# Layer 1's sliding-window scores: fp32 matmuls on 32-row tiles in place of stacked high and low halves, with the value projection moved to second place

## The chip, the cores and the metric

The kernel runs on one core of a Trainium2 chip. Its time is the device time of one execution in microseconds (us); three executions took 1122.43, 1123.97 and 1125.91 us, median 1123.97 us. The profile was taken of a further execution of 1124.34 us, whose span on the core is 1122.6 us. Engines are called as the profile calls them: PE (TensorE, matmuls), PEld (its weight loads), DVE (VectorE), ACT (ScalarE), POOL (GpSimd), SP (which issues most DMAs).

## The reference, cut to what matters

One inference step of a two-layer decoder for 256 prompt rows and 64 sample rows, all in float32. The part that is changed is layer 1's sliding-window attention over the prompt: 16 query heads in 4 groups per key head, 4 key heads, head size 64, window 128, with a learned sink per head.

```python
qp, kp, vp = odd_qkv(hp, pos_p, w_qkv_o[j], b_qkv_o[j])          # projection, bias, rotary on q and k
op = window_attn_prompt(qp, kp, vp, sinks[j]) @ w_out_o[j] + b_out_o[j]
...
def sink_attention(q, k, v, valid, sinks):
    s = jnp.einsum('...qkgd,...skd->...kgqs', q, k).astype(jnp.float32) * (C_HEAD_DIM ** -0.5)
    s = jnp.where(valid, s, -jnp.inf)
    sink = jnp.broadcast_to(sinks.astype(jnp.float32).reshape(C_KV_HEADS, C_GROUP, 1, 1), s.shape[:-1] + (1,))
    p = jax.nn.softmax(jnp.concatenate([s, sink], axis=-1), axis=-1)[..., :-1]
    return jnp.einsum('...kgqs,...skd->...qkgd', p.astype(v.dtype), v)
```

The 256 prompt queries are two blocks of 128. A query of block n sees keys of block n and of block n-1; block 0 has no block before it.

## The kernel before, in words

**Projections.** Every weight matrix is read in pieces of 128 x 2048 from one array (`ws`), in the order of a list (`plan`), through three `stage` buffers. Each piece is split into a high half rounded to fp32r (`whi`, written by ACT) and the rest (`wlo`, subtracted by DVE), in two parts of 1024 columns with four buffers each. The activations are split in the same way (`XH`, `XL`; later `HH`, `HL`). `gemm2` multiplies one piece with three fp32r matmuls per product (high x high, high x low, low x high), 48 matmuls a call, and calls `evac` at its end; `gemm_tok` does the same with positions on the partitions (24 matmuls per 512-wide piece, 64 for the value projection `w_qkv 5`). When a piece starts, the next one is split.

**Hooks.** Side work is put between the matmuls of the projections: `hook(i, f, j)` runs f inside the i-th following call, after the j-th of its 16 steps (a step is 3 matmuls in `gemm2`). PE, DVE, ACT and POOL each work through their own list strictly in the order that the compiled program has, so an instruction that waits holds all behind it on that engine. The order on each engine is made when the program is built, from priorities and an estimate of readiness.

**Layer 1, in the order of the program.** `qk_group(4)` makes the keys (one half of each head's 64 features on a chunk: chunk 8 holds features 0-31 of the four key heads in four bands of 32 partitions, chunk 9 features 32-63), `qk_group(0..3)` the queries of group g of all four key heads (chunks 2g, 2g+1 of the tile `QA`, called `k` in the profile since it lies in the buffer `k10`). Its `evac` scales on DVE (2 `t<-mm,RB`), rotates (4 `t<-t,cv,cst` on DVE, a subtract and an add `k<-t,t` on POOL). Then `gemm_tok` makes the values `VW` (in the buffer `cst`).

**Scores.** `stack_k` and `stack_q` build operands with 128 rows out of the 64 features: first `hilo` (ACT rounds, DVE subtracts), then ACT and DVE copy bands of 32 partitions so that one band holds a high half, the next a low half. For the keys this is the tile `khl` (buffer `k8b`), for the queries `sq` (buffer `Z`). A head's scores are then two fp32r matmuls of 128 rows and 256 columns (`at<-k8b,Z`). `w1` is one unit of 2 or 4 heads: matmuls into `at` banks (four PSUM banks), `tensor_tensor_reduce` on DVE (mask and row maximum; CUSTOM_DVE_ANT_0 in the profile, ISA in the program), `sink_softmax` (ACT exponentials, small DVE operations, DVE scaling). `w2f` transposes the probabilities on PE (`at<-ident,w`), `w3` multiplies them with the values (`at<-w,cst`), and ACT and DVE write high and low halves of the result to `OH`, `OL`. There are 12 units, in slots of two: slot i runs `w3` of the units two slots back, `w2f` of those one slot back, `w1` of its own. The slots lie in hooks from the value projection on, through `mem1.mk(0..3)` (memory keys, 48 matmuls of 256 columns each) and the pieces of `mem1.mv` (memory values, 24 matmuls of 512 columns each). `ws_prep`, `ws_scores`, `ws_tr`, `ws_pv` are the sample rows' attention; they stay as they are.

Of the kernel before, what the change touches and what calls it, by code (L numbers as in the profile page):

```python
# [9 lines left out]
F32 = mybir.dt.float32  # L10
F32R = mybir.dt.float32r
I32 = mybir.dt.int32
AF = mybir.ActivationFunctionType
# [62 lines left out]
def decoder_step(ctx: ExitStack, tc: tile.TileContext, d, plan):  # L76
# [968 lines left out]
    m1 = coc("m1")  # L1045
    VW = cst1[:, COW:COW + 768].rearrange("p (b c) -> p b c", b=3)
    bv = coc("bv")
    khl = sb([P, 2, 4, 256], "k8b", 1, F32R)

    def qk_group(g):  # L1050
        def evac(ps):
# [13 lines left out]
            V.scalar_tensor_tensor(q, zb, bb, cosw, op0=ALU.add, op1=ALU.mult)  # L1065
            G.tensor_tensor(QA[:, 2 * g + 1], p, q, op=ALU.add)
        gemm2(("w_qkv", g), nm.h, nm.l, NT, evac)

    def hilo(src, w):
        hi = sb([P, 512], "w2", W2, F32R)[:, :w]  # L1070
        lo = sb([P, 512], "w2", W2, F32R)[:, :w]
        if len(src.shape) == 3:
            hi = hi.rearrange("p (g t) -> p g t", g=src.shape[1])
            lo = lo.rearrange("p (g t) -> p g t", g=src.shape[1])
        A.activation(hi, src, AF.Copy)
        V.tensor_tensor(lo, src, hi.bitcast(F32), op=ALU.subtract)
        return hi.bitcast(F32), lo.bitcast(F32)

    def stack_k():
        for f in range(2):  # L1080
            hl = hilo(QA[:, 8 + f, :NPR], NPR)
            for kv in range(4):
                r = slice(32 * kv, 32 * kv + 32)
                for x in range(2):
                    for du in range(2):
                        q = (f + 2 * du) * 32
                        if du:
                            V.tensor_copy(khl[q:q + 32, x, kv], hl[x][r])
                        else:
                            A.activation(khl[q:q + 32, x, kv], hl[x][r], AF.Copy)  # L1090

    sq_t = {}

    def stack_q(gp, fs=(0, 1)):
        if 0 in fs:
            sq = sb([P, 2080], "Z", 1, F32R)[:, :2048].rearrange("p (k g t) -> p k g t", k=4, g=2)
            sq_t[gp] = sq
        sq = sq_t[gp]
        for f in fs:
            hl = hilo(QAv[:, 2 * gp:2 * gp + 2, f, :NPR], 512)  # L1100
            for kv in range(4):
                r = slice(32 * kv, 32 * kv + 32)
                for x in range(2):
                    q = (f + 2 * x) * 32
                    if x:
                        V.tensor_copy(sq[q:q + 32, kv], hl[x][r])
                    else:
                        A.activation(sq[q:q + 32, kv], hl[x][r], AF.Copy)

    isc = 0.125  # L1110
    OH = sb([P, KC, NT], "HH", 2, F32R)
# [2 lines left out]
    def sink_softmax(s, nh, mx, nsk, sk, sums, per):  # L1114
        nm_ = sb([P, nh], "w_nm", 4)
        es = sb([P, nh], "w_es", 4)
        if per:
            V.scalar_tensor_tensor(nm_, mx, -isc, nsk, op0=ALU.mult, op1=ALU.min)
        else:
            V.tensor_scalar(nm_, mx, -isc, nsk, op0=ALU.mult, op1=ALU.min)  # L1120
        for h in range(nh):
            A.activation(s[:, h], s[:, h], AF.Exp, bias=nm_[:, h:h + 1], scale=isc, accum_out=sums[:, h:h + 1])
        if per:
            V.tensor_tensor(es, nm_, sk, op=ALU.add)
            A.activation(es, es, AF.Exp)
# [7 lines left out]
    units = []  # L1133
    for gp in range(2):
        for pr in range(2):
            units.append((0, gp, pr, None))
        for kv in range(4):
            units.append((1, gp, kv // 2, kv))
    us, up_, uo = {}, {}, {}

    def w1(u):
        n, gp, pr, kv = units[u]
        heads = [(k, g) for k in ((2 * pr, 2 * pr + 1) if n == 0 else (kv,)) for g in range(2)]
        nh = len(heads)
        kw = 512 // nh
        s = sb([P, 512], "w2", W2).rearrange("p (h k) -> p h k", k=kw)
        mx = sb([P, nh], "w_mx", 4)
        msk = m1[:, P:256] if n == 0 else m1
        for j, (k, g) in enumerate(heads):
            if j % 2 == 0:  # L1150
                sp = bank("at")
            o = (j % 2) * 256
            for x in range(2):
                T.matmul(sp[:, o:o + 256], sq_t[gp][:, k, g, n * P:(n + 1) * P], khl[:, x, k],
                         start=(x == 0), stop=(x == 1))
            V.tensor_tensor_reduce(out=s[:, j], in0=sp[:, o:o + kw], in1=msk, op0=ALU.add, op1=ALU.max,
                                   scale=1.0, scalar=NEG, accum_out=mx[:, j:j + 1])
        sums = sb([P, nh], "w_sm", 4)
        if n == 0:
            for i in range(2):  # L1160
                i0 = CV["sink_p"][0] - CV["sink_s"][0] + (2 * pr + i) * 4 + 2 * gp
                sink_softmax(s[:, 2 * i:2 * i + 2], 2, mx[:, 2 * i:2 * i + 2], nsink[:, i0:i0 + 2],
                             cvc("sink_p", (2 * pr + i) * 4 + 2 * gp, 2), sums[:, 2 * i:2 * i + 2], True)
        else:
            i0 = CV["sink_p"][0] - CV["sink_s"][0] + kv * 4 + 2 * gp
            sink_softmax(s, 2, mx, nsink[:, i0:i0 + 2], cvc("sink_p", kv * 4 + 2 * gp, 2), sums, True)
        us[u] = s

    def w2f(u):
        n, gp, pr, kv = units[u]  # L1170
        s = us.pop(u)
# [8 lines left out]
        up_[u] = pt  # L1180

    def w3(u):
        n, gp, pr, kv = units[u]
        pt = up_.pop(u)
        first = n == 0 or kv % 2 == 0
        if first:
            uo[n, gp, pr] = bank("at")
        po = uo[n, gp, pr]
        for i in range(2):
            k = 2 * pr + i if n == 0 else kv  # L1190
            ro = slice((k % 2) * 64, (k % 2) * 64 + 64)
            kb = 0 if n == 0 else i
            T.matmul(po[ro, :256], VW[:, kb, k * 64:(k + 1) * 64], pt[:, i * 256:(i + 1) * 256],
                     start=(n == 0 or i == 0), stop=(n == 0 or i == 1))
        if n == 0 or kv % 2 == 1:
            src = po[:, :256].rearrange("p (g q) -> p g q", g=2)
            c0 = pr * 4 + 2 * gp
            oh = OH[:, c0:c0 + 2, n * P:(n + 1) * P]
            A.activation(oh, src, AF.Copy)
            V.tensor_tensor(OL[:, c0:c0 + 2, n * P:(n + 1) * P], src, oh.bitcast(F32), op=ALU.subtract)  # L1200

    sm_ = {}

# [81 lines left out]
    def slot(i):  # L1285
        for u in (2 * i - 4, 2 * i - 3):
            if 0 <= u < 12:
                w3(u)
        for u in (2 * i - 2, 2 * i - 1):
            if 0 <= u < 12:  # L1290
                w2f(u)
        for u in (2 * i, 2 * i + 1):
            if u < 12:
                w1(u)

    def rows_out():
        G.dma_start(d["wk_p"], QA[:, 8:10, P:2 * P])
        G.dma_start(d["wk_n"], QA[:, 8:10, NPR:NT])
        G.dma_start(d["wv_p"], VW[:, 1])
        G.dma_start(d["wv_n"], VW[64:128, 2])  # L1300

    qk_group(0)
    hook(0, stack_k)
    qk_group(1)
    hook(0, lambda: stack_q(0, (0,)))
    hook(1, lambda: stack_q(0, (1,)))
    qk_group(2)
    qk_group(3)
    hook(0, lambda: slot(0))
    gemm_tok([("w_qkv", 5)], nm.h, nm.l, XS, 256, evac)  # L1310
    hook(0, lambda: slot(1), rows_out)
    hook(1, lambda: slot(2), lambda: stack_q(1))
    hook(2, ws_prep, lambda: slot(3))
    hook(3, lambda: slot(4))
    for g in range(4):
        mem1.mk(g)
    hook(0, lambda: slot(5), lambda: ws_scores(0))
    hook(1, lambda: slot(6), lambda: ws_scores(1))
    hook(2, lambda: slot(7), lambda: ws_tr(0))
    hook(3, lambda: ws_tr(1), j=3)  # L1320
    hook(3, ws_pv, j=11)
    mem1.mv(0)
# [47 lines left out]
def _plan():  # L1370
# [243 lines left out]
```

## Time and profile before

| what | value |
|---|---|
| runs | 1122.43, 1123.97, 1125.91 us (median 1123.97) |
| profiled execution | 1124.34 us, span 1122.6 us |
| PE busy | 1086.4 us, 97% of the span |
| DVE, ACT, POOL busy | 738.8 (66%), 524.2 (47%), 136.3 us (12%) |
| layer 1 from the end of its norm to the last `mem1.mv` matmul | 634.95 to 759.64 us of the span |
| DVE busy from 640 to 660 us | 19.77 of 20.00 us |

PE is busy nearly all the time, so the time of the kernel is PE's list of matmuls plus the places where PE stands still or runs at half its clock. The profile writes an fp32 matmul as two records, an fp32r matmul as one; a record's own duration contains a tail that overlaps the next one, so what a matmul costs is read from the distance between starts. "Idle" in brackets is the time that an engine stood before an instruction, and the name behind the arrow what ended it.

### The profile page before, as it was taken

The page shows a single profiled execution, that of the slowest core. Times are in us where ns is not written, and L with a number is a line of the kernel's source. Part 1 is how long each engine was busy: PE and PEld are TensorE (multiplying, and loading weights), DVE is VectorE, ACT ScalarE, POOL GpSimd, SP SyncE. Part 2 cuts the span into 40 slices and gives each one's busy share as a digit, 9 for nine tenths or more (in the row PEclk, how much of TensorE's full clock was granted, in tenths as well). Part 3 has the DMA queues.
Part 4 walks back from the last instruction along what each step waited for, and adds up shares of the span by engine and source line. Part 5 has one row for each costly group of instructions (what it writes and reads, how often), then busy time and mean ns, then how long its engine had stood idle before and what let it go on. Part 6 is the DMA issues. An engine that isn't in the chain of part 4 may idle for free.

```text
span 1122.6 us, 18500 instructions
## 1 busy us (share of the span) xinstructions
PE 1086.4 (97%) x7424; PEld 1021.9 (91%) x7424; DVE 738.8 (66%) x1447; ACT 524.2 (47%) x910; POOL 136.3 (12%) x131
## 2 busy tenths in 40 slices
PE   7998999999999999999999989999999999999996
PEld 7886979999987999999999988879968999999995
DVE  8999885776545575555556898956536855555543
ACT  6454641545325355444445557745323654343432
POOL 4506030123000010000001222002000200000001
PEclk9999999999999999999999989999999999999998
DMA  9432337744787644444444334547576444444421
GB/s 349 146 128 98 131 119 271 287 148 152 296 328 309 263 151 150 151 150 151 150 151 150 121 113 156 188 149 278 209 300 264 149 150 151 150 151 150 151 75 48
DMA packets 30982, 201.55 MB, mean 180 GB/s; under 512 B 3624, under 2 KB 4792, under 8 KB 7992
## 3 DMA queue, kind: packets, MB, share of 16 engines
q1 hardware_dynamic: 27584, 187.13, 45.8%
q0 software_dynamic: 2512, 11.54, 2.8%
q10 hardware_dynamic: 800, 1.70, 0.5%
q8 instruction: 58, 0.95, 0.3%
q14 instruction: 28, 0.23, 0.1%
HBM read 187.51 MB, written 12.85 MB: 178 GB/s over the span
## 4 chain that ended last, share of the span: by engine, by line
PE 74%; DVE 13%; DMA 5%; ACT 4%; issue 2%; POOL 1%; SPq 0%; ACTq 0%; DVEq 0%; POOLq 0%
PE mm L64 64%; PE at L64 10%; DVE wlo L64 5%; DMA stage<-ws 4%; DVE t L64 2%; ACT whi L64 2%; DVE w L64 1%; POOL t L64 1%; DVE XL L64 1%; ACT w L64 1%; ACT k L64 1%; DVE Z L64 0%; DVE k8b L64 0%; DVE nw_u L64 0%; DVE X L64 0%
## 5 line engine op out<-in xcount | busy, mean ns | idle before, releaser
L64 DVE TENSOR_TENSOR wlo<-stage,whi 128x1024 fp32r<-128x1024 f32 (+1 forms) x270 | 339.5, 1264 | 191.6 <-ACT whi L64 189.9
L64 ACT ACTIVATE whi<-stage 128x1024 fp32r<-128x1024 f32 (+1 forms) x270 | 280.2, 1050 | 363.5 <-PE mm L64 273.4
L64 PE MATMUL mm<-HH,whi 128*128 128x320 f32 (+1 forms) x960 | 294.4, 308 | 2.2 <-ACT HH L64 2.2
L64 PE MATMUL mm<-HL,whi 128*128 128x320 f32 (+1 forms) x960 | 293.8, 306 | 0.3 <-DVE HL L64 0.2
L64 PE MATMUL mm<-HH,wlo 128*128 128x320 f32 (+1 forms) x960 | 293.3, 306 | 0.0
L64 PE MATMUL mm<-XH,whi 128*128 128x320 f32 x912 | 286.9, 315 | 5.3 <-ACT whi L64 5.3
L64 PE MATMUL mm<-XH,wlo 128*128 128x320 f32 x912 | 283.9, 311 | 5.5 <-DVE wlo L64 5.3
L64 PE MATMUL mm<-XL,whi 128*128 128x320 f32 x912 | 283.4, 311 | 0.0
L64 PEld LDWEIGHTS mm<-HH,whi 128*128 128x128 f32 x960 | 180.7, 188 | 4.9 <-ACT HH L64 2.4
L64 PEld LDWEIGHTS mm<-HL,whi 128*128 128x128 f32 x960 | 181.0, 189 | 1.0 <-DVE HL L64 0.8
L64 PEld LDWEIGHTS mm<-HH,wlo 128*128 128x128 f32 x960 | 180.9, 188 | 0.1
L64 PEld LDWEIGHTS mm<-XH,whi 128*128 128x128 f32 x912 | 172.8, 189 | 6.9 <-ACT whi L64 5.3
L64 PEld LDWEIGHTS mm<-XH,wlo 128*128 128x128 f32 x912 | 172.6, 189 | 6.7 <-DVE wlo L64 6.7
L64 PEld LDWEIGHTS mm<-XL,whi 128*128 128x128 f32 x912 | 172.8, 189 | 0.7
L64 POOL TENSOR_TENSOR ssq<-ssq,sqt 128x320 f32<-128x320 f32 x39 | 41.6, 1068 | 609.0 <-ACT sqt L64 608.1
L64 DVE TENSOR_TENSOR X<-mm,X 128x320 f32<-128x320 f32 x112 | 51.7, 488 | 56.8 <-PE mm L64 56.6
L64 ACT ACTIVATE t<-t 128x320 f32<-128x320 f32 x88 | 38.0, 462 | 24.1 <-DVE t L64 24.1
L64 DVE SCALAR_TENSOR_TENSOR t<-mm,RB 128x320 f32<-128x320 f32 x64 | 30.1, 491 | 25.5 <-PE mm L64 22.6
L64 ACT ACTIVATE HH<-t 128x320 fp32r<-128x320 f32 x80 | 34.5, 462 | 21.6 <-DVE t L64 21.1
L64 DVE TENSOR_TENSOR HL<-t,HH 128x320 fp32r<-128x320 f32 x80 | 37.0, 491 | 9.9 <-ACT HH L64 9.3
L64 DVE SCALAR_TENSOR_TENSOR XL<-X,cv,XH 128x320 fp32r<-128x320 f32 x48 | 38.4, 822 | 4.7 <-ACT XH L64 4.7
L64 ACT ACTIVATE XH<-X,cv 128x320 fp32r<-128x320 f32 x48 | 26.3, 554 | 21.1 <-DVE X L64 19.3
(240 smaller groups left out, 1139.3 us busy)
## 6 DMA issues: line engine op xcount, KB each, us to landing
stage<-ws SPq DMA_DIRECT2D x162, 1024.0 KB, 4.8
o_ret_s<-stage POOLq DMA_DIRECT2D x8, 512.0 KB, 6.9
HH<-ws SPq DMA_DIRECT2D x4, 1024.0 KB, 6.8
HL<-ws SPq DMA_DIRECT2D x4, 1024.0 KB, 6.6
k8a<-ws SPq DMA_DIRECT2D x2, 1024.0 KB, 8.3
o_mem_k<-k8a POOLq DMA_DIRECT2D x2, 1024.0 KB, 8.2
o_mem_v<-k8b POOLq DMA_DIRECT2D x2, 1024.0 KB, 10.6
cst<-ce SPq DMA_DIRECT2D x1, 1296.0 KB, 10.3
```

The costliest lines, as they stand in the source:

```text
L64: r = f(*a, **k)
```

## The change

Nothing is split and stacked any more. The scores are plain fp32 matmuls straight from `QA`: for one group g and one half f, four matmuls, one for each key head, each with 32 rows (its band of partitions) and 128 weight columns, into a bank of their own; f = 0 and f = 1 accumulate. `w1` now does all four key heads at once, in three calls: block 1 with groups 0 and 1, block 0 with all four groups, block 1 with groups 2 and 3. It takes all four `at` banks, and its softmax writes to one big tile (`k8b`, `Z`, `k8b`). Block 0 computes 128 columns of scores where it had computed 256 and read 128. `w3` handles two key heads at once. The value projection is second in the plan, before the queries, and the hooks are laid out anew.

```diff
-    khl = sb([P, 2, 4, 256], "k8b", 1, F32R)
...
-    def hilo(src, w):
-        hi = sb([P, 512], "w2", W2, F32R)[:, :w]
-        lo = sb([P, 512], "w2", W2, F32R)[:, :w]
...
-        A.activation(hi, src, AF.Copy)
-        V.tensor_tensor(lo, src, hi.bitcast(F32), op=ALU.subtract)
...
-    def stack_k():
-        for f in range(2):
-            hl = hilo(QA[:, 8 + f, :NPR], NPR)
...
-    def stack_q(gp, fs=(0, 1)):
...
-            hl = hilo(QAv[:, 2 * gp:2 * gp + 2, f, :NPR], 512)
...
-    def w1(u):
...
-            for x in range(2):
-                T.matmul(sp[:, o:o + 256], sq_t[gp][:, k, g, n * P:(n + 1) * P], khl[:, x, k],
-                         start=(x == 0), stop=(x == 1))
...
+    def w1(n, gp, tag):
+        gs = range(4) if n == 0 else (2 * gp, 2 * gp + 1)
+        kw = 512 // len(gs)
+        sp = [bank("at") for _ in range(4)]
+        for j, g in enumerate(gs):
+            for f in range(2):
+                for kv in range(4):
+                    r = slice(32 * kv, 32 * kv + 32)
+                    T.matmul(sp[kv][:, j * kw:(j + 1) * kw], QAv[r, g, f, n * P:(n + 1) * P], QA[r, 8 + f, :kw],
+                             start=(f == 0), stop=(f == 1))
+        big = sb([P, 2080 if tag == "Z" else 2048], tag)
...
+        for kv in range(4):
+            s = big[:, kv * 512:(kv + 1) * 512].rearrange("p (h k) -> p h k", k=kw)
...
+    def w3(n, gp, pr):
+        po = bank("at")
+        ng = 4 if n == 0 else 2
+        w = ng * P
+        pts = [up_.pop((n, gp, 2 * pr + i)) for i in range(2)]
+        for kb in range(n + 1):
+            for i in range(2):
+                k = 2 * pr + i
+                T.matmul(po[i * 64:i * 64 + 64, :w], VW[:, kb, k * 64:(k + 1) * 64], pts[i][:, kb * w:(kb + 1) * w],
+                         start=(kb == 0), stop=(kb == n))
...
-    qk_group(0)
-    hook(0, stack_k)
-    qk_group(1)
-    hook(0, lambda: stack_q(0, (0,)))
-    hook(1, lambda: stack_q(0, (1,)))
-    qk_group(2)
-    qk_group(3)
-    hook(0, lambda: slot(0))
     gemm_tok([("w_qkv", 5)], nm.h, nm.l, XS, 256, evac)
-    hook(0, lambda: slot(1), rows_out)
...
+    hook(2, lambda: w1(1, 0, "k8b"), j=9)
+    hook(3, lambda: w2f(1, 0, 0), lambda: w2f(1, 0, 1), j=9)
+    hook(4, lambda: w3(1, 0, 0), lambda: w2f(1, 0, 2), lambda: w2f(1, 0, 3), rows_out, j=3)
+    hook(4, lambda: w1(0, 0, "Z"), j=13)
+    hook(5, lambda: w3(1, 0, 1), ws_prep, j=5)
+    hook(6, lambda: w2f(0, 0, 0), lambda: w2f(0, 0, 1), j=3)
...
+    hook(7, lambda: w1(1, 1, "k8b"), j=9)
+    for g in range(4):
+        qk_group(g)
     for g in range(4):
         mem1.mk(g)
...
-    p += [("w_qkv", 4), ("w_qkv", 0), ("w_qkv", 1), ("w_qkv", 2), ("w_qkv", 3), ("w_qkv", 5)]
+    p += [("w_qkv", 4), ("w_qkv", 5), ("w_qkv", 0), ("w_qkv", 1), ("w_qkv", 2), ("w_qkv", 3)]
```

On PE, before, the first scores stand inside the value projection (`mm` from `whi`, `wlo` and `XH`, `XL`); each row here is one unit's pair of heads, and its operands are the stacked tiles.

```order
L64 MATMUL mm_6683<-wlo_6599,XH_5982 128x256
L64 MATMUL mm_6683<-whi_6598,XL_5983 128x256
L64 MATMUL at_6721<-k8b_6217,Z_6545 128x256 x2
L64 MATMUL at_6728<-k8b_6217,Z_6545 128x256 x2
L64 MATMUL at_6760<-k8b_6217,Z_6545 128x256 x2
L64 MATMUL at_6767<-k8b_6217,Z_6545 128x256 x2
L64 MATMUL mm_6682<-whi_6602,XH_5982 128x256
```

Now they stand inside `qk_group(2)`, 30 of whose 48 matmuls are ahead of them: 16 matmuls in one block (this row of four, four times over), with `QA` (`k`) as both operands and a bank for each key head.

```order
L64 MATMUL mm_6563<-XL_5983,whi_6484 128x320
L64 MATMUL mm_6563<-XH_5982,wlo_6485 128x320
L64 MATMUL at_6594<-k_945_6216 128x256
L64 MATMUL at_6595<-k_945_6216 128x256
L64 MATMUL at_6596<-k_945_6216 128x256
L64 MATMUL at_6597<-k_945_6216 128x256
```

The scores moved from behind all four query groups to the middle of the third, and no longer read `k8b` and `Z`.

On DVE, before, this is what stands ahead of the first scores: the evacuation of `qk_group(2)`, the low half of the stacked queries (`w<-k`), splits of weights (`wlo`) and the copies to `Z`.

```order
L64 TENSOR_TENSOR wlo_6603<-stage_6596,whi_6602 128x1024
L64 SCALAR_TENSOR_TENSOR t_1014_6592<-t_1010_6583,cv_62,cst_6211 128x320
L64 TENSOR_TENSOR w_1023_6633<-k_945_6216,w_1022_6632 128x512
L64 TENSOR_TENSOR wlo_6688<-stage_6685,whi_6687 128x1024
L64 CAST Z_6545<-w_1023_6633 32x512 x4
L64 TENSOR_TENSOR t_1024_6668<-mm_6606,RB_6329 128x320
```

Now, ahead of the first scores and behind them, with the evacuation of `qk_group(1)` first and the softmax of block 1 (ISA rows) last:

```order
L64 TENSOR_TENSOR t_998_6538<-mm_6488,RB_6329 128x320
L64 TENSOR_TENSOR t_999_6539<-mm_6489,RB_6329 128x320
L64 SCALAR_TENSOR_TENSOR t_1000_6542<-t_998_6538,cv_62,cst_6211 128x320
L64 SCALAR_TENSOR_TENSOR t_1001_6543<-t_999_6539,cv_62,cst_6211 128x320
L64 SCALAR_TENSOR_TENSOR t_1002_6547<-t_998_6538,cv_62,cst_6211 128x320
L64 TENSOR_TENSOR wlo_6559<-stage_6552,whi_6558 128x1024
L64 SCALAR_TENSOR_TENSOR t_1003_6548<-t_999_6539,cv_62,cst_6211 128x320
L64 TENSOR_TENSOR wlo_6710<-stage_6707,whi_6709 128x1024
L64 ISA k8b_6614,w_mx_6615<-at_6594,cst_6211 128x256
```

The subtractions and copies are gone from this list, and DVE goes from an evacuation straight to the softmax.

On POOL, now, `ws_prep` (MEMSET and COPY of `XH`) lies between and around the two operations that finish the queries of group 3 (`t_1051` to `t_1054`), behind those of group 2:

```order
L64 TENSOR_TENSOR k_945_6216<-t_1036_6702,t_1037_6703 128x320
L64 MEMSET XH_7041 128x2048
L64 TENSOR_TENSOR k_945_6216<-t_1051_6785,t_1052_6786 128x320
L64 COPY XH_7041<-k_945_6216 32x8x32 x4
L64 TENSOR_TENSOR k_945_6216<-t_1053_6790,t_1054_6791 128x320
L64 COPY XH_7041<-k_945_6216 32x8x32 x4
```

Before, all ten `k<-t,t` of POOL came ahead of this MEMSET and its copies.

## Rows read from the trace of the kernel before

**Rows 1.** The page: each engine's busy time, share, instructions.
```profile
PE 1086.4 (97%) x7424; PEld 1021.9 (91%) x7424; DVE 738.8 (66%) x1447; ACT 524.2 (47%) x910; POOL 136.3 (12%) x131
```
**Rows 2.** Waits of PE, 634.6 to 759.6: us in total, times, longest.
```profile
PE at L64 <- DVE Z L64: 4.7, 2, 3.8
PE at L64 <- DVE w_mx L64: 1.1, 1, 1.1
PE mm L64 <- DVE t L64: 0.7, 1, 0.7
```
**Rows 3.** Stretches: us, busy PE, PEld, DVE, ACT, POOL, PEclk, DMA, GB/s.
```profile
640.00:660.00 20.00, 20.00 (x139) 20.00 (x138) 19.77 (x38) 15.40 (x27) 6.60 (x7) 1.00 0.32 107
661.55:664.50 2.95, 2.95 (x24) 2.89 (x24) 2.95 (x5) 2.90 (x4) 1.12 (x1) 1.00 0.01 3
668.46:674.35 5.89, 5.89 (x26) 5.67 (x26) 5.80 (x11) 0.00 (x0) 1.13 (x2) 0.51 0.11 45
819.40:842.40 23.00, 22.23 (x239) 13.87 (x242) 10.46 (x48) 7.75 (x26) 0.00 (x0) 1.00 0.81 315
```
**Rows 4.** PE in order of time: start, us, instruction [idle before].
```profile
634.95 0.55 PE L64 MATMUL mm<-XH,whi 128*128 128x320 f32 x1
...
668.46 0.77 PE L64 MATMUL at<-k8b,Z 128*128 128x256 f32 x2 [3.82 <-DVE Z L64]
...
707.18 1.45 PE L64 MATMUL at<-k8b,Z 128*128 128x256 f32 x10
708.48 0.28 PE L64 MATMUL mm<-HH,whi 128*128 128x256 f32 x1
...
819.43 1.93 PE L64 MATMUL at<-stage,Z 128*32 128x256 f32 x32
821.29 3.72 PE L64 MATMUL at<-k8a,k 128*128 128x256 f32 x16
```
**Rows 5.** DVE in order of time, ahead of the first scores.
```profile
667.90 0.87 DVE L64 CAST Z<-w 32x512 fp32r<-32x512 f32 x2
```
**Rows 6.** Groups on DVE, 636 to 710: count | busy us, mean ns | idle.
```profile
L64 DVE TENSOR_TENSOR wlo<-stage,whi 128x1024 fp32r<-128x1024 f32 x14 | 22.6, 1619 | 0.5 <-ACT whi L64 0.4
L64 DVE SCALAR_TENSOR_TENSOR t<-t,cv,cst 128x320 f32<-128x320 f32 x20 | 10.1, 545 | 0.0
L64 DVE CAST Z<-w 32x512 fp32r<-32x512 f32 x16 | 6.7, 420 | 0.4
L64 DVE TENSOR_TENSOR t<-mm,RB 128x320 f32<-128x320 f32 x10 | 4.4, 484 | 1.5 <-ACT RB L64 1.4
L64 DVE CUSTOM_DVE_ANT_0 w<-at,cst 128x256 f32<-128x256 f32 x8 | 3.1, 420 | 0.5 <-PE at L64 0.4
L64 DVE TENSOR_SCALAR w<-w,w_sm 128x256 f32<-128x256 f32 x8 | 2.5, 350 | 0.1
L64 DVE SCALAR_TENSOR_TENSOR w_nm<-w_mx,nsink 128x2 f32<-128x2 f32 x12 | 1.7, 155 | 0.0
```
**Rows 7.** PE in order of time: short matmuls, value products, transposes.
```profile
690.46 1.08 PE L64 MATMUL at<-w,cst 128*64 128x256 f32 x8
691.47 1.09 PE L64 MATMUL at<-ident,w 128*128 128x128 f32 x8
...
727.20 0.66 PE L64 MATMUL at<-stage,XH 128*128 128x128 f32 x4
727.70 0.56 PE L64 MATMUL at<-k,XH 128*128 128x64 f32 x4
728.09 0.66 PE L64 MATMUL at<-stage,XH 128*128 128x128 f32 x4
```
**Rows 8.** Groups on POOL, 636 to 715, with the same columns.
```profile
L64 POOL TENSOR_TENSOR k<-t,t 128x320 f32<-128x320 f32 x10 | 10.9, 1087 | 38.7 <-DVE t L64 38.7
L64 POOL COPY XH<-k 32x256 f32<-32x256 f32 x8 | 3.5, 440 | 0.4
L64 POOL MEMSET XH<- 128x2048 f32 x1 | 1.8, 1810 | 1.0 <-PE mm L64 1.0
```

More of the change, by code (lines that the diff above doesn't have):

```diff
@@ L1067, in qk_group @@
         gemm2(("w_qkv", g), nm.h, nm.l, NT, evac)
-    def hilo(src, w):
-        hi = sb([P, 512], "w2", W2, F32R)[:, :w]
-        lo = sb([P, 512], "w2", W2, F32R)[:, :w]
-        if len(src.shape) == 3:
-            hi = hi.rearrange("p (g t) -> p g t", g=src.shape[1])
-            lo = lo.rearrange("p (g t) -> p g t", g=src.shape[1])
-        A.activation(hi, src, AF.Copy)
-        V.tensor_tensor(lo, src, hi.bitcast(F32), op=ALU.subtract)
-        return hi.bitcast(F32), lo.bitcast(F32)
-    def stack_k():
-        for f in range(2):
-            hl = hilo(QA[:, 8 + f, :NPR], NPR)
-            for kv in range(4):
-                r = slice(32 * kv, 32 * kv + 32)
-                for x in range(2):
[L1085 to L1092, printed above, removed]
-    def stack_q(gp, fs=(0, 1)):
[L1095 to L1099, printed above, removed]
-            hl = hilo(QAv[:, 2 * gp:2 * gp + 2, f, :NPR], 512)
[L1101 to L1108, printed above, removed]
     isc = 0.125
@@ L1131, in sink_softmax @@
             V.tensor_scalar(s[:, h], s[:, h], sums[:, h:h + 1], None, op0=ALU.mult)
[L1133 to L1136, printed above, removed]
-        for kv in range(4):
-            units.append((1, gp, kv // 2, kv))
-    us, up_, uo = {}, {}, {}
-    def w1(u):
[L1142 to L1153, printed above, removed]
-                T.matmul(sp[:, o:o + 256], sq_t[gp][:, k, g, n * P:(n + 1) * P], khl[:, x, k],
-                         start=(x == 0), stop=(x == 1))
[L1156 to L1167, printed above, removed]
@@ L1169, in w2f @@
-    def w2f(u):
-        n, gp, pr, kv = units[u]
-        s = us.pop(u)
+    us, up_, uo = {}, {}, {}
+    def w1(n, gp, tag):
[9 more added lines that the diff above has]
+        big = sb([P, 2080 if tag == "Z" else 2048], tag)
+        msk = m1[:, P:256] if n == 0 else m1
+        nh = len(gs)
+        for kv in range(4):
+            s = big[:, kv * 512:(kv + 1) * 512].rearrange("p (h k) -> p h k", k=kw)
+            mx = sb([P, nh], "w_mx", 4)
+            for j in range(nh):
+                V.tensor_tensor_reduce(out=s[:, j], in0=sp[kv][:, j * kw:(j + 1) * kw], in1=msk, op0=ALU.add,
+                                       op1=ALU.max, scale=1.0, scalar=NEG, accum_out=mx[:, j:j + 1])
+            sums = sb([P, nh], "w_sm", 4)
+            i0 = CV["sink_p"][0] - CV["sink_s"][0] + kv * 4 + gs[0]
+            sink_softmax(s, nh, mx, nsink[:, i0:i0 + nh], cvc("sink_p", kv * 4 + gs[0], nh), sums, True)
+            us[n, gp, kv] = s
@@ L1172, in w2f @@
+    def w2f(n, gp, kv):
+        s = us.pop((n, gp, kv))
         tp = bank("at")
@@ L1179, in w2f @@
         A.activation(pt, tp, AF.Copy)
[L1180 to L1200, printed above, removed]
+        up_[n, gp, kv] = pt
+    def w3(n, gp, pr):
[8 more added lines that the diff above has]
+                         start=(kb == 0), stop=(kb == n))
+        src = po[:, :w].rearrange("p (g q) -> p g q", g=ng)
+        c0 = pr * 4 + 2 * gp
+        oh = OH[:, c0:c0 + ng, n * P:(n + 1) * P]
+        A.activation(oh, src, AF.Copy)
+        V.tensor_tensor(OL[:, c0:c0 + ng, n * P:(n + 1) * P], src, oh.bitcast(F32), op=ALU.subtract)
     sm_ = {}
@@ L1283, in evac @@
         V.scalar_tensor_tensor(VW[64:128, 2], fs, nm.rs[64:128, 2:3], bv[64:128], op0=ALU.mult, op1=ALU.add)
[L1285 to L1294, printed above, removed]
     def rows_out():
@@ L1300, in rows_out @@
         G.dma_start(d["wv_n"], VW[64:128, 2])
-    qk_group(0)
-    hook(0, stack_k)
-    qk_group(1)
-    hook(0, lambda: stack_q(0, (0,)))
-    hook(1, lambda: stack_q(0, (1,)))
-    qk_group(2)
-    qk_group(3)
-    hook(0, lambda: slot(0))
-    gemm_tok([("w_qkv", 5)], nm.h, nm.l, XS, 256, evac)
-    hook(0, lambda: slot(1), rows_out)
-    hook(1, lambda: slot(2), lambda: stack_q(1))
-    hook(2, ws_prep, lambda: slot(3))
-    hook(3, lambda: slot(4))
+    gemm_tok([("w_qkv", 5)], nm.h, nm.l, XS, 256, evac)
+    hook(2, lambda: w1(1, 0, "k8b"), j=9)
[4 more added lines that the diff above has]
+    hook(6, lambda: w2f(0, 0, 0), lambda: w2f(0, 0, 1), j=3)
+    hook(6, lambda: w3(0, 0, 0), lambda: w2f(0, 0, 2), lambda: w2f(0, 0, 3), j=13)
+    hook(7, lambda: w3(0, 0, 1), j=3)
+    hook(7, lambda: w1(1, 1, "k8b"), j=9)
+    for g in range(4):
+        qk_group(g)
     for g in range(4):
         mem1.mk(g)
-    hook(0, lambda: slot(5), lambda: ws_scores(0))
-    hook(1, lambda: slot(6), lambda: ws_scores(1))
-    hook(2, lambda: slot(7), lambda: ws_tr(0))
+    hook(0, lambda: ws_scores(0), j=5)
+    hook(1, lambda: w2f(1, 1, 0), lambda: w2f(1, 1, 1), j=1)
+    hook(1, lambda: w3(1, 1, 0), lambda: w2f(1, 1, 2), lambda: w2f(1, 1, 3), lambda: ws_scores(1), j=9)
+    hook(2, lambda: w3(1, 1, 1), lambda: ws_tr(0))
     hook(3, lambda: ws_tr(1), j=3)
```

## The prediction

> **What bounds the kernel now.** I read the busy times first. PE works 97% of the span [rows 1], so the time changes by what PE's list costs and by where PE stands still or runs slowly; work saved on ACT or DVE counts only where PE waits for it. The waits of PE come second. In the stretch that the change touches, the three largest are 4.7 us for the copies to `Z`, 1.1 for a row maximum, 0.7 for an evacuation [rows 2], together 6.5 us. Then the stretches: from 640 to 660 us DVE is busy 19.77 of 20.00 us [rows 3]. PE reaches the first scores, which need `Z`, and stands 3.82 us [rows 4] until DVE has done the copies of the second half, the last two starting at 667.90 [rows 5]. The clock is the fourth view. Behind that pause the granted clock of PE is 0.51 for 5.89 us, that is 1.2 GHz instead of 2.4; ahead of the pause it is 1.00 [rows 3].
>
> **The change, part by part.**
>
> *Stacking goes.* The 16 copies to `Z` alone are 6.7 us of DVE [rows 6], and the copies to `khl`, the rounding on ACT and the subtractions go as well. PE gets back what it waited for them: I count all 6.5 us of [rows 2], since the row maximum and the evacuation were late in the same full DVE list.
>
> *The slow clock goes with the pause.* The 5.89 us hold 26 records: 8 score matmuls and 18 of the value projection. At the full clock a score record costs 0.13 us (ten between 707.18 and 708.48, [rows 4]) and one of the projection 0.123 (24 in 2.95, [rows 3]): 1.0 + 2.2 = 3.2 us. That gives back 2.7 us.
>
> *The score matmuls.* Before: 64 records at 0.13 = 8.3 us at full clock. After: `w1` for block 1 has 16 fp32 matmuls of 256 columns, four at a time on different bands of 32 rows, twice; for block 0 it has 32 of 128 columns. The trace has no matmul of 32 rows, so I bound it. If the four row tiles run at once, the nearest row is that of 128 x 32 column tiles, where four fp32 matmuls of 256 columns also go to four tiles: 32 records, which is 16 matmuls, take 821.29 - 819.43 = 1.86 us [rows 4]. That is one `w1` of block 1 exactly; block 0 has twice the records of half the length and I give it the same. Sum 3 x 1.86 = 5.6 us. If they run one after the other, an fp32 record of 256 columns costs 0.23 us (16 in 3.72, [rows 4]) and one of 128 columns 0.125 (four from 727.20 to 727.70, [rows 7]): 64 x 0.23 + 64 x 0.125 = 22.7 us. I take 5.6, since the column tiles have the same instruction, the same length and the same four-way choice of tile, and keep 22.7 as the far end. The gain is 8.3 - 5.6 = 2.7 us. While those column tiles ran, from 819.40 to 842.40, the granted clock stayed at 1.00 [rows 3], so I charge nothing for the clock.
>
> The Trainium skill (TensorE: Matmul & The Clock Gate, Measured speedup vs the span model) gives four row tiles of 32 rows at 512 columns a measured 3.07 times, not four. By it the scores would cost 22.7 / 3.07 = 7.4 us, and the sum would be 1.8 us smaller.
>
> *Value products and transposes.* The number of transposes is the same, 48. The value products cover the same columns in pairs of column tiles, as before (four in 1.08 us, [rows 7]); I count them at nothing. Two key heads are now in one call of `w3`, which waits for both; both come out of the same `w1`.
>
> *The value projection second.* It costs the same 64 matmuls. It takes the place of `qk_group(0)` while the norm's factors are on their way; its own factors come from the same short chain. Its evacuation lies on DVE where DVE then waits for `qk_group(0)`, so that is its cover. SP's loads keep their order and number, but for that one piece.
>
> *The new waits.* The three blocks of scores need finished queries from POOL, and the transposes need a finished softmax from DVE. I lay the lists end to end from 634.95 [rows 4], with 0.145 us for a matmul of 320 columns (139 in 20.00) and 0.123 for one of 256 [rows 3]. The rest of the projection is 43 x 0.123, which gives 640.2; two query groups give 654.1; 30 matmuls of the third give 658.5, the first `w1`. DVE starts the evacuation of `qk_group(1)` at 654.1: 2 x 0.44 + 3 x 0.5 + a split of 1.6 + 0.5 = 4.5 us [rows 6], then POOL's add of 1.1 [rows 8]: 659.7. Only the last 4 of the 16 score matmuls need that add; the first 12 keep PE until 659.9. No wait, by 0.2 us.
>
> Softmax, in the order on DVE up to the second key head: 8 x 0.39 + 4 x 0.31 + 0.44 + 10 short operations of 0.14 [rows 6] = 6.2, from 660.4 to 666.6. PE comes to the first transposes after 48 x 0.145, at 667.4. Again no wait, by 0.8.
>
> The rest of that softmax and the evacuation of `qk_group(2)` take 4 x 0.31 + 0.44 + 4 x 0.5 + 0.8 = 4.5, to 671.1; two splits 3.2; `qk_group(3)`: 0.9 + 1.5 + a split 1.6 + 0.5, to 678.8. On POOL the add of group 2 ends at 672.2 and the MEMSET at 674.0; the subtract of group 3 ends at 677.3, four copies at 679.1, the add at 680.2 [rows 8]. On PE: 667.4 + 1.0 for the transposes + 18 x 0.145 + 12 x 0.123 + 1.1 + 1.0 + 30 x 0.123 = 678.3, then 28 of the 32 short matmuls 1.6: 679.9. A wait of 0.3 us.
>
> The third `w1` comes some 20 us later, with none of this in front of it. Since two margins of three are under 0.3 us, I charge 0.8 us in all. `w1` holds all four `at` banks; the next user on PE comes after at least 18 + 6 matmuls of `mem1.mk` (2.9 us), when DVE has long read the first bank (four maxima), so I charge nothing for that.
>
> The Trainium skill (TensorEngine Tiling (Array Packing), Gotcha 1: PSUM Pressure) says that row tiles raise the pressure on PSUM, since each needs a bank of its own. By it the next user of a bank would be late, but with the 2.9 us above it changes no term.
>
> *Sum.* 6.5 + 2.7 + 2.7 - 0.8 = 11.1 us off the profiled execution: 1124.34 - 11.1 = 1113.2. That execution is 0.4 us above the median of the runs, so against the median I forecast 1112.9 us.
>
> **The rivals.**
>
> *A. The row tiles run one after the other, so the change doesn't do what it says.* For it: no row shows a matmul of 32 rows sharing the array with another, and all weights have 128 columns here where the column tiles have 32. Against it: different tiles start together in the rows of column tiles. The scores would cost 22.7 instead of 5.6: 1112.9 + 17.1 = 1130.0, slower by 6. It turns slower once the three blocks cost over 5.6 + 11.1 = 16.7 us.
>
> *B. The matmuls run at once but the weight loads queue.* A record of 64 columns still costs 0.098 us (four from 727.70 to 728.09, [rows 7]), although its columns are half those of the one at 0.125: a floor that looks like the weight load's. 128 loads at 0.098 are 12.5 us, 6.9 more than I counted: 1119.8.
>
> The Trainium skill (TensorE: Matmul & The Clock Gate, LDWEIGHTS (loading the stationary operand)) says that a load of 32 x 128 takes as long as one of 128 x 128, because columns set its time; by that rule B holds if the loads of different row tiles don't overlap. The same page (Part 3, The mechanism) lets loads overlap matmuls of other row groups, and no run here shows either yet.
>
> *C. DVE and POOL come late and the wait moves rather than goes.* For it: between 654 and 680 DVE has no idle time in my layout, so each microsecond that it runs late reaches PE at the block of group 3 or at the transposes. Its splits cost 1.6 on average but 22.6 us hold slow ones [rows 6], and POOL's MEMSET and copies now stand between the two operations on group 3. Against it: it loses over 6.7 us of copies. If both places are 2 us late, and one pause brings the slow clock back (2.7), that is 6.7 - 0.8 = 5.9 more: 1118.8.
>
> **How the numbers follow.** Forecast as summed, 0.64; B or something between, 0.12; C, 0.13; A, 0.11. A measurement of this kernel tells a change from none at about 0.3%, 3.4 us, so faster means under 1120.6. The forecast's own spread is from 1109.5 (no new waits, and a tail of overlaps that I counted as cost) to 1116. B and C end inside "faster" in most of their spread, in part at no change. Faster 0.64 + 0.09 + 0.09 = 0.82; no change 0.08 (upper ends of B and C, A by half); slower 0.10. The range 1109 to 1120.5 takes in the forecast, C and most of B, and leaves A out.
>
> **What would show it.** In the profile after: the four matmuls of a set starting within some nanoseconds of each other, the next set 0.2 us later (A: 0.23 between single records); three blocks of about 1.9 us; no wait of PE over 1 us from 635 to 750; PEclk 1.00 throughout; the last `mem1.mv` matmul near 748.5 instead of 759.64. The forecast is wrong if the blocks take over 3 us each, if PE waits for POOL `k` or DVE `k8b` or `Z` for several us, or if what is saved here comes back as a wait for a transfer behind 760, of which I see no sign, since the loads are released by PE's own progress.

## The result and the profile after

| | before | changed |
|---|---|---|
| median of the runs made side by side | 1124.72 us (1122.43 to 1125.91) | 1111.92 us (1111.58 to 1113.89) |
| ratio, 95% interval | | 0.989 (0.9875 to 0.9905) |
| profiled execution, span | 1124.34 us, 1122.6 us | 1111.76 us, 1110.1 us |

The changed kernel is faster by 1.1%, 1.0 us below the forecast of 1112.9 us. The engines' line of the page after, against [rows 1]:

```profile
PE 1080.7 (97%) x7480; PEld 1015.9 (92%) x7480; DVE 717.9 (65%) x1391; ACT 504.3 (45%) x866; POOL 139.0 (13%) x131
```

PE is busy 5.7 us less, DVE 20.9 and ACT 19.9 us less; PE's share is 97% as before, so only its list, its waits and its clock matter, and DVE's gain counts through the waits alone. What is left of PE's waits, against [rows 2]; first the wait itself (total, times, longest), from 634 to 747 us:

```profile
PE at L64 <- POOL k L64: 0.9, 1, 0.9
```

To compare the two kernels I cut a stretch that is the same work in both: from the first matmul of the norm's sums (`at<-ones,ssq`) to the first of the output projection. Its row after (stretch, us, busy time of PE, PEld, DVE, ACT, POOL, granted clock, DMA, GB/s):

```profile
628.19:747.03 118.84, 117.92 (x898) 105.08 (x897) 88.88 (x263) 59.23 (x148) 24.80 (x27) 1.00 0.46 159
```

And here is the same stretch before:

```profile
629.53:759.64 130.11, 123.29 (x842) 110.97 (x841) 108.96 (x319) 79.41 (x192) 22.51 (x27) 0.97 0.43 145
```

The stretch is 11.27 us shorter, PE's idle time in it fell from 6.82 to 0.92, and its granted clock is 1.00 instead of 0.97. It starts 1.34 us earlier after, although PE's list ahead of it is the same: over this study's ten profiled executions its start lay anywhere from 627.86 to 632.06 us. So 11.3 us of the difference of spans (12.5) belong to the change, and the rest is spread of the executions. Below, kernels are compared by the length of this stretch, which is free of that spread, and by the medians beside it.

The three score blocks on PE after (start, us, instruction, idle before), against [rows 4]; the row behind each block shows where it ends, and the last row is the end of the stretch:

```profile
657.46 2.01 PE L64 MATMUL at<-k 32*128 32x256 f32 x32
659.39 0.41 PE L64 MATMUL mm<-XH,whi 128*128 128x320 f32 x1
...
677.16 1.84 PE L64 MATMUL at<-k 32*128 32x128 f32 x56
679.92 0.50 PE L64 MATMUL at<-k 32*128 32x128 f32 x8 [0.92 <-POOL k L64]
680.36 0.39 PE L64 MATMUL mm<-HH,whi 128*128 128x256 f32 x1
...
701.54 2.01 PE L64 MATMUL at<-k 32*128 32x256 f32 x32
703.48 0.39 PE L64 MATMUL mm<-HH,whi 128*128 128x256 f32 x1
...
747.03 0.31 PE L64 MATMUL mm<-HH,whi 128*128 128x320 f32 x1
```

The blocks cost 1.93, 2.28 (3.20 less the wait) and 1.94 us: 6.15 us for all scores, which before took 9.60 between starts. The wait stands where the last eight records, group 3's second half, need POOL's add. POOL around it:

```profile
670.77 1.81 POOL L64 MEMSET XH<- 128x2048 f32 x1
673.72 2.25 POOL L64 TENSOR_TENSOR k<-t,t 128x320 f32<-128x320 f32 x1 [1.13 <-DVE t L64]
676.03 2.90 POOL L64 COPY XH<-k 32x256 f32<-32x256 f32 x4
679.01 0.86 POOL L64 TENSOR_TENSOR k<-t,t 128x320 f32<-128x320 f32 x1
```

The add has no idle time in front of it: it comes late because four copies for the sample rows are ahead of it in POOL's list.

### The profile page after: what moved, and what is told of

It is laid out like the page before. It is cut to its first block, busy times and chain, and to the rows that moved or that the text cites. A ratio compares the mean times of both kernels' runs of the same rounds, so it can differ in the third digit from the quotient of the medians.

```text
span 1110.1 us, 18507 instructions
## 1 busy us (share of the span) xinstructions
PE 1080.7 (97%) x7480; PEld 1015.9 (92%) x7480; DVE 717.9 (65%) x1391; ACT 504.3 (45%) x866; POOL 139.0 (13%) x131
## 4 chain that ended last, share of the span: by engine, by line
PE 76%; DVE 12%; DMA 4%; ACT 3%; issue 2%; POOL 2%; SPq 0%; ACTq 0%; DVEq 0%; POOLq 0%
PE mm L64 66%; PE at L64 10%; DVE wlo L64 4%; DMA stage<-ws 4%; DVE t L64 2%; ACT whi L64 1%; POOL t L64 1%; DVE XL L64 1%; DVE k8b L64 1%; DVE w L64 1%; ACT k L64 1%; DVE nw_u L64 0%; ACT w L64 0%; DVE X L64 0%; ACT XH L64 0%
```

## The experiments

The theory to test: the gain is (a) the pause for the stacked copies and the smaller waits, (b) the slow clock behind that pause, (c) cheaper scores because four row tiles run at once; the order of the value projection gives nothing. All stretches in one table (median of the runs, ratio to the kernel before on the same chip, stretch as defined above):

| kernel | median us | ratio, 95% interval | stretch us |
|---|---|---|---|
| before | 1124.72 | | 130.11 |
| changed | 1111.92 | 0.989 (0.9875 to 0.9905) | 118.84 |
| band by band | 1126.6 | 1.0026 (1.001 to 1.0042) | 133.43 |
| values last | 1113.86 | 0.9905 (0.9874 to 0.9935) | 118.47 |
| before, no stacking | 1116.07 | 0.9929 (0.9903 to 0.9955) | 121.61 |
| scores twice | 1116.85 | 0.9939 (0.992 to 0.9957) | 122.95 |
| pause, not held | 1112.78 | 0.9913 (0.9889 to 0.9936) | 119.69 |
| POOL's add first | 1111.87 | 0.9907 (0.9878 to 0.9937) | 117.71 |
| halves inside | 1111.87 | 0.9897 (0.9871 to 0.9923) | 119.04 |
| pause held | 1118.6 | 0.9948 (0.993 to 0.9965) | 124.74 |

**Band by band.** The matmuls are the same, but they are issued one key head after the other.

```diff
-        for j, g in enumerate(gs):
-            for f in range(2):
-                for kv in range(4):
+        for kv in range(4):
+            for j, g in enumerate(gs):
+                for f in range(2):
```

> The same 128 records of scores as in the changed kernel, issued in another order: all matmuls of one key head (one band of 32 rows) one behind the other, then the next key head. Theory (the four row tiles share the array only when neighbours in PE's list stand on different bands): the three blocks cost 22.7 us (64 records of 256 columns at 0.23, 64 of 128 at 0.125) instead of the 6.2 us read from the changed kernel, so 1111.9 + 16.5 = 1128.4 us, slower than before by about 4. Rival (a matmul of 32 rows is cheap by itself, and the order does not matter): 1111.9 us, within 2. In between (neighbours overlap only at the seams of the bands, or weights load ahead): about 1120.

Measured 1126.6 us, slower than before, so the order of PE's list alone decides over the whole gain. The first two blocks on PE:

```profile
659.12 4.91 PE L64 MATMUL at<-k 32*128 32x256 f32 x32
...
681.73 8.99 PE L64 MATMUL at<-k 32*128 32x128 f32 x64
690.65 0.58 PE L64 MATMUL mm<-HH,whi 128*128 128x256 f32 x1
```

Then the stretches with the first block, the second, and the one behind it:

```profile
659.10:664.00 4.90, 4.90 (x34) 4.17 (x33) 4.12 (x16) 1.71 (x7) 0.82 (x1) 1.00 0.62 214
...
681.73:690.65 8.92, 8.92 (x65) 8.70 (x64) 5.53 (x38) 4.70 (x25) 2.22 (x4) 0.69 0.04 15
690.65:695.80 5.15, 5.15 (x27) 5.02 (x26) 4.73 (x25) 3.19 (x13) 0.00 (x0) 0.54 0.00 0
```

The blocks cost 4.84, 8.92 and 4.84 = 18.6 us, 12.45 more than in the changed kernel. That is under the 22.7 expected, because bands still overlap at their seams: in the trace the second band's first record (478 ns long, as the first one of each band is, where the others have 374) starts at 660.098 us, together with the fifth of the first band's eight (660.092), so half of a band runs beside the next one. In the second block it starts at 683.179, together with the thirteenth of the first band's sixteen (683.173). And the slow clock adds to it: the clock falls in the second block though PE never stands still (8.92 of 8.92 us busy), which costs 2.8 of its 8.92 us (8.92 x (1 - 0.69)), and what stands behind it takes 2.4 us longer than in the changed kernel. 12.45 + 2.4 + 0.65 (a later wait for ACT) - 0.92 (no wait for POOL) = 14.6, which is the difference of the stretches.

**Values last.** The value projection goes behind the four query groups again, in the plan and in the code, and the hooks from the first value product on move one call.

```diff
-    gemm_tok([("w_qkv", 5)], nm.h, nm.l, XS, 256, evac)
...
     for g in range(4):
         qk_group(g)
+    gemm_tok([("w_qkv", 5)], nm.h, nm.l, XS, 256, evac)
```

> The changed kernel with the value projection behind the four query groups again, as before the change; scores, hooks and their distance to the query groups as in the changed kernel, except that everything from the first value product on comes one call later. Theory (the order of the value projection is worth nothing by itself): 1111.9 us, within 1.5; the wait for POOL at the block of four groups (0.9 us) goes, since 7.9 us of value projection now stand ahead of it, so 1111.0 if anything. Rival (the move carries a part of the gain, because DVE has the value evacuation early where it waits anyway): 1114 to 1119, with a wait of PE of 2 us or more between 640 and 690.

The stretch is 118.47 us, 0.37 shorter than in the changed kernel. The median, 1113.86 us (1109.21 to 1115.12), is 1.9 above that kernel's and does not go against it: in the profiled execution the stretch starts at 632.06 us, the latest of all, and 1.9 us is within that spread. The wait at the block of four groups is gone as expected; a wait of 0.59 us, which was not expected, stands in the first block instead (PE at both blocks):

```profile
655.82 0.71 PE L64 MATMUL at<-k 32*128 32x256 f32 x8 [0.59 <-POOL k L64]
681.81 2.07 PE L64 MATMUL at<-k 32*128 32x128 f32 x64
```

The rival is out: by the stretch, the move carries no part of the gain.

**Before, without stacking.** This is the kernel before, with its copies left out; its scores read the memory activations, so they are not those of the reference.

```diff
-    hook(0, stack_k)
...
-    hook(0, lambda: stack_q(0, (0,)))
-    hook(1, lambda: stack_q(0, (1,)))
...
-                T.matmul(sp[:, o:o + 256], sq_t[gp][:, k, g, n * P:(n + 1) * P], khl[:, x, k],
+                T.matmul(sp[:, o:o + 256], mem1.mh[:, 2 * k + g, n * P:(n + 1) * P], mem1.ml[:, 2 * k + x, :NPR],
```

> The kernel before, with the stacked copies left out (rounding, subtractions and band copies for keys and queries): its score matmuls, same number, shape and type, read the memory activations instead, which are ready long before, so the scores are not those of the reference. The value projection stays last. Theory (the change gains 9.2 us from the pause for the copies, the smaller waits and the slow clock behind the pause, and 2.7 us from cheaper scores): 1124.7 - 9.2 = 1115.5 us, no wait of PE over 1 us between 635 and 710, granted clock 1.00 throughout. Rival (the gain is the cheaper scores and the order of the value projection; without stacking another item of DVE's list is late in its place): 1120 to 1124.7 us, with a pause for a row maximum or an evacuation at the first scores.

1116.07 us for 1115.5 expected. The stretch is 8.50 us shorter than before and 2.77 longer than the changed kernel's, where 9.2 and 2.7 were expected. Its waits of PE from 634 to 765 us:

```profile
PE at L64 <- DVE w_mx L64: 1.0, 2, 0.5
```

And its stretch with the first scores, with the columns of the stretches above:

```profile
664.00:679.00 15.00, 13.97 (x115) 13.39 (x114) 14.20 (x54) 7.98 (x26) 9.78 (x13) 1.00 0.39 137
```

The clock is 1.00 where it was 0.51 [rows 3]. DVE is still busy 14.20 of 15.00 us there, and two waits of 0.5 us for a row maximum stay: so not all waits of [rows 2] that are not for `Z` went with the copies. In the changed kernel they are gone.

**Scores twice.** Each group's eight matmuls are issued twice.

```diff
-        for j, g in enumerate(gs):
+        for j, g in [(j, g) for j, g in enumerate(gs) for _ in range(2)]:
```

> The changed kernel with each group's eight score matmuls issued twice (the second time over the first, so the values are the same). It prices the score blocks on the path. Theory (they cost what the trace shows and nothing covers them): 6.2 us more, 1111.9 + 6.2 = 1118.1 us, each block of 3.9 to 4.6 us instead of 1.9 to 2.3. Rival (their true price is in the switches between large and small tiles, not in the records): 1 to 2 us more, about 1113.5. Rival B of the prediction (weight loads queue once more of them follow each other): 128 more loads at 0.098 us, 12.5 us more, 1124.4.

The median is 1116.85 us, and the stretch is 4.1 us longer: 4.96 for the second issue, where 6.2 was expected, less the 0.9 of the wait, which is gone here. The two shapes of block:

```profile
679.95 3.85 PE L64 MATMUL at<-k 32*128 32x128 f32 x128
683.73 0.39 PE L64 MATMUL mm<-HH,whi 128*128 128x256 f32 x1
704.97 3.73 PE L64 MATMUL at<-k 32*128 32x256 f32 x64
708.63 0.39 PE L64 MATMUL mm<-HH,whi 128*128 128x256 f32 x1
```

A block of 256 columns goes from 1.94 to 3.66 us: the four sets added cost 0.43 us each. One matmul of that shape on 128 rows costs 0.43 as well: the 16 records of `at<-k8a,k` in [rows 4] start 0.216 us apart once they run (the first takes 0.32), and a matmul is two records. So a set of four costs as much as one, and some 0.2 us a block is start and end. That is a factor of 4 from set to set, and of 16 x 0.43 / 1.94 = 3.6 for a whole block. The Trainium skill (TensorE: Matmul & The Clock Gate, Measured speedup vs the span model) gives 3.07 for four row tiles at 512 columns; here the measurement decides. 128 records of 128 columns take 3.78 us, 0.030 each, a third of the 0.098 that rival B charged, so the loads of different bands don't queue. The first rival (the price is in the switches) would have added 1 to 2 us and is out too.

**Pause put back.** The first block stands early in the third query group, with the matmuls that need POOL's last add in front.

```diff
-    hook(2, lambda: w1(1, 0, "k8b"), j=9)
+    hook(2, lambda: w1(1, 0, "k8b", 1), j=0)
...
-        for j, g in enumerate(gs):
-            for f in range(2):
+        for j, g in list(enumerate(gs))[::-1 if rev else 1]:
+            for f in ((1, 0) if rev else (0, 1)):
```

> The changed kernel with its first score block three matmuls into the third query group instead of thirty, and with the matmuls that need POOL's last add of the second group in front. In the changed kernel's trace the block would then stand ready at 653.5 us and that add ends at 658.3: one pause of PE of about 4.8 us, with no stacking, no fp32r scores and no other instruction added. Theory (the slow clock in the kernel before was the price of the pause itself): the granted clock falls to about 0.5 behind the pause and some 6 us of work take twice as long, so 4.8 + 2.7 = 7.5 us more, less the 0.9 us wait that may go: 1118.5 to 1119.4 us. Rival (the slow clock came from something else in the kernel before, such as the stacked fp32r scores or the full DVE): 1.00 behind the pause, 4.8 us more at most: 1116 to 1116.7.

The condition was missed: the order made at build time kept 28 matmuls of the third group ahead of the block instead of 3, and the pause was 1.08 us instead of 4.8. PE at the block:

```profile
660.78 0.50 PE L64 MATMUL at<-k 32*128 32x256 f32 x4 [1.08 <-POOL k L64]
```

And the stretch behind it, whose clock column is the third from the end:

```profile
660.00:667.00 7.00, 6.22 (x61) 5.82 (x62) 5.82 (x30) 3.02 (x14) 0.73 (x1) 1.00 0.41 150
```

Behind this pause of 1.08 us the clock stays at 1.00. Of a long one the run says nothing; the next run has it.

**Pause held.** This is the same kernel, with PE held to the program's order through the third group.

```diff
+        InOrder.pe = g == 2
         qk_group(g)
+        InOrder.pe = False
```

> The run with the pause put back, once more: there PE's list had the block behind 28 matmuls of the third group instead of 3, so the pause was 1.1 us and not 4.8, and the granted clock stayed at 1.00. Now PE's list is held in the order of the program through that group, and three matmuls stand ahead of the block; nothing else differs. Theory (the slow clock in the kernel before was the price of a pause of that length): one pause of 4.5 to 5 us before the first score block, then a granted clock of about 0.5 for some 6 us: 4.8 + 2.7 = 7.5 us more in the stretch than in the changed kernel (118.8 us from the norm's first sum to the first matmul of the output projection), so 126.3, and 1118.5 to 1119.4 us. Rival (the slow clock needs something else of the kernel before): the clock stays at 1.00, 4.8 us more: 123.6 in the stretch, 1116.7 us.

The median is 1118.6 us, as the theory had it, but the stretch, 124.74 us, lies between the theory's 126.3 and the rival's 123.6, so the clock itself has to decide. PE at the block:

```profile
660.56 3.80 PE L64 MATMUL at<-k 32*128 32x256 f32 x32 [4.72 <-POOL k L64]
664.29 0.64 PE L64 MATMUL mm<-XH,whi 128*128 128x320 f32 x1
```

And four stretches of 2 us from the block on:

```profile
660.00:662.00 2.00, 1.44 (x12) 1.22 (x16) 0.00 (x0) 0.00 (x0) 0.51 (x1) 0.50 0.91 270
662.00:664.00 2.00, 2.00 (x24) 1.41 (x16) 0.00 (x0) 0.00 (x0) 0.00 (x0) 0.50 0.64 262
664.00:666.00 2.00, 2.00 (x12) 1.71 (x9) 1.62 (x11) 0.39 (x1) 0.00 (x0) 0.69 0.00 0
666.00:668.00 2.00, 2.00 (x16) 2.00 (x15) 1.92 (x14) 2.00 (x11) 0.00 (x0) 1.00 0.00 0
```

The same 32 records take 3.73 us instead of 1.93 at a granted clock of 0.50. The stretch is 5.9 us longer: 4.72 of pause, 1.8 in the block and some 0.5 in the projection behind it, less the 0.92 of the wait for POOL, which is gone here, and 0.3 in the second block, which runs undivided. So a pause alone brings the slow clock, with no stacking and no stacked score in the program; it cost 2.3 us where 2.7 was expected. The rest of what is missing to 126.3 are the 0.92 and the 0.3, which the expectation had left out.

**POOL's add first.** The eight copies are kept in program order, half 1 first, so that all of them come behind the add.

```diff
-        for f in range(2):
+        for f in (1, 0):
...
-    hook(5, lambda: w3(1, 0, 1), ws_prep, j=5)
+    hook(5, lambda: w3(1, 0, 1), lambda: in_order(ws_prep), j=5)
```

> The changed kernel with POOL's eight small copies for the sample rows all behind the add that finishes the queries of the last group (half 1 is copied first, in program order); PE's list is the same. Theory (the 0.9 us wait at the second score block is those four copies, 2.9 us on POOL in the trace, standing ahead of the add): the add comes 2.9 us earlier, no wait of PE on POOL is left between 635 and 750, 0.9 us less: about 1111.0 us, too little for the times to tell, so the trace decides. Rival (the add itself is late because DVE delivers its inputs late): the wait stays at 0.5 to 0.9 us, with DVE as the one that POOL waits for.

No wait of PE is left from 634 to 765 us, and the stretch is 117.71 us, 1.13 shorter than in the changed kernel. POOL:

```profile
673.41 1.12 POOL L64 TENSOR_TENSOR k<-t,t 128x320 f32<-128x320 f32 x1 [1.14 <-DVE t L64]
676.15 0.86 POOL L64 TENSOR_TENSOR k<-t,t 128x320 f32<-128x320 f32 x1 [1.62 <-DVE t L64]
677.08 4.32 POOL L64 COPY XH<-k 32x256 f32<-32x256 f32 x8
```

And the second block on PE, in one piece:

```profile
676.85 2.07 PE L64 MATMUL at<-k 32*128 32x128 f32 x64
678.84 0.39 PE L64 MATMUL mm<-HH,whi 128*128 128x256 f32 x1
```

So the copies ahead of the add were the cause of the wait. This is the best version by its stretch; its median (1111.87 us, 1110.29 to 1115.71) can't be told from the changed kernel's.

**Halves inside.** Two matmuls, which are four records, are issued on one band before the next.

```diff
-            for f in range(2):
-                for kv in range(4):
+            for kv in range(4):
+                for f in range(2):
```

> The changed kernel with the two halves of the features innermost: two matmuls (four records) on the same band of 32 rows, then the next band, instead of another band with each matmul. Theory, from the band-by-band run (there the second band started when the first had three or four records left, so PE seems to let a free band start past two or three records that wait for a busy one): blocks of 2.4 to 3.1 us instead of 1.9 to 2.3, 1 to 3 us more in all: 1113 to 1115. Rival 1 (only direct neighbours on different bands overlap): blocks of 4 us or more, 6 us more: 1118. Rival 2 (each band has a queue of its own, deep enough for four records): no change, 1111.9.

My theory, 2.4 to 3.1 us a block, fell. The second rival holds nearly: the first block goes from 659.35 to 661.40, 2.05 us instead of 1.93, and the stretch is 0.2 longer.

```profile
659.35 2.13 PE L64 MATMUL at<-k 32*128 32x256 f32 x32
...
661.40 0.42 PE L64 MATMUL mm<-XH,whi 128*128 128x320 f32 x1
```

Runs of four records on a band cost 0.12 us a block of 256 columns, runs of eight (band by band) 2.9. The picture that fits both is a band that lets three records wait behind the one that runs without stopping the others: band by band, the next band starts when three of the first are left, in runs of eight and of sixteen alike. It is argued from these two runs, and the depth was not measured by itself.

## Why the prediction was right

*The sum.* 11.1 us were forecast and the stretch gave 11.27. By time between starts, with what the prediction had in brackets: PE's idle time is 5.90 less (6.5 - 0.8 = 5.7); the scores go from 9.60 to 6.15 and the value projection from 7.79 to 6.05, together 5.19 less (2.7 + 2.7 = 5.4); `mem1.mv` goes from 23.67 to 23.09, which the prediction did not have; everything else is 0.4 longer. The last two nearly cancel, by luck. `mem1.mv` gains because its list is cut into fewer pieces: where one of its matmuls stands next to side work it can take 0.31 to 0.34 us instead of 0.23, and that is so 15 times before and 9 times after. The layout held too: moved by the 1.34 us of the earlier start, the first `w1` was forecast for 657.2 and stands at 657.46, block 0 for 677.0 and stands at 677.16. What the prediction and the table ahead of it call the last matmul of `mem1.mv` (759.64) is the first one of the output projection; it was forecast for 747.2 and stands at 747.03.

*The waits.* The 4.7 us for `Z` went, as the run without stacking shows, with only the operands of the scores changed beside it. That the row maximum's wait would go with the same DVE list was too simple: without stacking it stays at 1.0 us in the old slots, and it went only with the new layout.

*The slow clock.* The step was right, in size too: the slow part of the scores (0.9) and of the value projection (1.7) makes 2.6 us for 2.7. The held pause shows the cause.

*The score matmuls.* 8.3 to 5.6 was forecast. At full clock it was 8.7 to 6.15, so both ends were 0.4 to 0.55 low and nearly cancel. The first was low because in twelve of the small units the first score matmul takes 0.19 to 0.22 us instead of 0.12, the second mainly because the block of 128 columns took 2.28 and not 1.86; undivided by a wait it takes 2.00, as the run with POOL's add first shows. The choice of the column tiles as the nearest row was right, and rivals A and B are out. A's price was too high in the blocks (18.6, not 22.7), in part because a record on 128 rows costs 0.216 by starts and not the 0.23 that holds its tail, and it left out the clock; its sign was right. The row tiles are not all of this gain, though: block 0 is also narrowed from 256 to 128 columns. With 256 it would be 64 records of that length, which take 3.66 us in the run with the scores twice, so I estimate 1.4 us of the 2.5 for the narrowing. What it would have saved with stacked operands no run shows.

*The value projection* in second place gains nothing, as forecast; the run with it last shows it.

*The new waits.* They were charged 0.8 us in all, and 0.92 was found in one place, at the block of group 3 as laid out, where 0.3 was worked out. That the total fits is luck, since the layout failed on POOL: its four copies took 2.90 us against 4 x 0.44 [rows 8] and the subtract 2.25 against 1.1. The trace shows what stands beside them: the subtract (673.72 to 675.97) and the one slow copy each lie across a split of weights on DVE.

```profile
674.02 1.21 DVE L64 TENSOR_TENSOR wlo<-stage,whi 128x1024 fp32r<-128x1024 f32 x1
...
677.03 1.21 DVE L64 TENSOR_TENSOR wlo<-stage,whi 128x1024 fp32r<-128x1024 f32 x1
677.06 1.43 POOL L64 COPY XH<-k 32x256 f32<-32x256 f32 x1
```

The other three copies took 0.39 to 0.56 us. In the run with POOL's add first the subtract took 1.12 us, and there the split beside it is the longer one:

```profile
673.72 1.89 DVE L64 TENSOR_TENSOR wlo<-stage,whi 128x1024 fp32r<-128x1024 f32 x1
```

So in these places either POOL's instruction or the split beside it comes out long, and the layout had priced POOL without DVE. What the two share is not shown. There is no wait at the first block, where the add ends at 658.26 and the first of the four matmuls that need it starts at 658.64 (0.4 us, forecast 0.2), and none at the transposes, for which the second key head is ready at 664.6 and which start at 666.5 (1.9 us, forecast 0.8). Rival C did not come: one wait of 0.92 us brought no slow clock.

*Behind the stretch* nothing came back: from the first matmul of the output projection to the end of the span it is 362.96 us before (1122.6 - 759.64) and 363.07 after.

## What to carry to other kernels

Small contractions of 32 rows can be had at the price of one in four if PE's list changes the band at least every second fp32 matmul; the same matmuls in band order cost three times as much and lose the whole gain. When a wait of PE is removed, price what stands behind it as well: here pauses of 3.82 and 4.72 us cost 2.6 and 2.3 us more in slow clock, and those up to 1.08 us nothing. And when a result moves to the front of a path, look through the list of the small engine that finishes it, since unrelated copies may stand ahead of it.

## What the runs showed of the hardware that I had not expected

The granted clock fell without any pause. In the band-by-band run PE is busy 8.92 of 8.92 us in the second block and the clock is 0.69 there and 0.54 in the 5.15 us behind it, while the same 64 records with the bands interleaved, and twice as many of them (3.78 us), leave it at 1.00. Why it falls there stays open.

A row tile does not need direct neighbours to overlap: a second band starts while three records of the first, ahead of it in PE's list, have not started (660.098 beside 660.092 us, above). So matmuls on different bands can start out of the order of that list, which the text ahead of the prediction calls strict. And four row tiles at once come at the whole factor: they cost 0.43 us a set, as one matmul of all 128 rows does.

POOL and DVE seem to hold each other up: a subtract on POOL took 2.25 us and a copy 1.43 beside splits on DVE, against 1.12 and 0.39 elsewhere, and where the subtract took 1.12 the split beside it took 1.89 instead of 1.21.
